# Opening broadcasts placed among squares and projections, weight tiles requested a tile ahead, scan tables two tiles later, in a one-core hybrid block

## The chip, the core and the metric

The kernel runs on one core of a Trainium2 chip. The time is device time in microseconds (us) of one execution. The core has five engines that work through queues of their own, each strictly in order, and wait for each other by semaphores: TensorE (PE in the profile, with its weight loads PEld) for matmuls, VectorE (DVE), ScalarE (ACT), GpSimd (POOL) and SyncE (SP), which here only issues transfers. Matmuls accumulate into PSUM, which has eight banks of 128 x 512 fp32; operands lie in SBUF.

## The reference, cut to what matters

One block over 256 tokens, D = 2048, fp32. The matrices are `w_in` (2048 x 8192), `w_glu`, two output projections, `w_out`, two MLP matrices of 4 x D, and `w_ada`, from which the modulation comes.

```python
mod = silu(c) @ w_ada + b_ada
sh1, sc1, g1, sh2, sc2, g2 = split(mod, 6)
h = rms_norm(x, norm_mix_g) * (1 + sc1) + sh1
u, q, k, v, ga, gb = split(h @ w_in, ...)
y_ssm = s5_branch(u, ...)          # scan, gelu: y; then y * sigmoid(y @ w_glu + b_glu)
y_att = moba_attention(q, k, v, rel_bias)
merged = sigmoid(ga) * (y_ssm @ w_proj_ssm) + sigmoid(gb) * (y_att @ w_proj_attn)
x = x + g1 * (merged @ w_out)
h2 = rms_norm(x, norm_mlp_g) * (1 + sc2) + sh2
x = x + g2 * (square(relu(h2 @ w_ff1)) @ w_ff2)
return rms_norm(x, norm_final_g)
```

## The kernel before

**Products.** Every fp32 product is made of three products in a shorter format: each operand is split into a high part (a cast) and a low part (the difference), and hi x hi, hi x lo and lo x hi are summed. A weight tile is 128 x 1024 fp32, 512 KB. `load` requests it on SP into one of seven buffers (`wraw`, L162 to L167). `split` makes `whi` by a cast on ACT (L172) and `wlo` by a subtraction on DVE (L174); each has four buffers. A tile then feeds either 24 matmuls of 256 columns (`steps_t`, output `pt`, L253 to L255) or 12 of 512 columns (`steps_n`, output `pn`, L309 to L313). `stream` walks over the tiles of a product; where `look` is set, it requests the next tile right after the split of the present one, once.

**Opening.** While x arrives in four pieces, the squares of x are taken on ACT, added up on DVE (`junk`, L520, L521) and summed over the features by matmuls with ones (`ss`, L523), for the norm R. `spread_c(b, gate)` (L1062) writes silu(c), spread over all partitions, into a bank `adab` by four matmuls against the identity; ACT copies it to `cb` (L1070). `cb` is later what DVE multiplies rows of `w_ada` with, to get the modulation as totals (`ada_wide`, L415, 2.3 us each). For the first feature tile the modulation comes from matmuls instead: `ada_first` (`adap`, L343), a copy (`s`, L347) and a transposing product (`adac`, L353). Matmuls that nobody reads (`idle`, L141) stand at the very start and behind `adac`. Then h of the first feature tile is made and the first matmul of the input projection can run.

**Input projection.** `w_in` is worked through by column groups of 1024 and by groups of 1, 3, 4 and 8 feature tiles, as h becomes ready: the list `order` names 15 pieces, and `duo` runs two of them interleaved by a pattern. Partial sums that do not fit into PSUM are copied to SBUF (`qk`, `v`, `uT`, `gp`, all on ACT, L1183) and copied back as seeds (L220: `pn<-v`, `pt<-qk`). The tiles are numbered here from 0 in the order in which they are loaded; tiles 7 to 10 are in the first `duo`, 17 to 27 in the second. h of later feature tiles is made on ACT (`htmp`, L545) and split.

**Attention and scan.** While PE works on the gate columns of `w_in` (four products of 16 tiles), work of the attention heads and then of the state-space scan is put between the tiles by "lanes": lists of jobs that are issued at a given rate per tile. `to_ssm`, called in the second gate product, finishes the heads that are left and puts the list `bgl` of the scan (tables, `ssm_in`, `ssm_scan`, `ssm_ys`, GELU, `hop_out`) in their place. Its end is `yT`, moved between partitions by transfers. `proj_attn(0)` follows (8 tiles of `w_proj_attn`; DVE multiplies the result into `gb`, L1364), then `yT` is split into `yy` (four casts, four subtractions, L172 and L174) and multiplied with `w_glu`.

**What sets the order.** The engines' queues are not written by hand: a scheduler in the framework places every instruction by its own estimate of times, from the order of the program, the priorities (`high_priority`) and the constraints given with `after`. So an edit in one place can move instructions far behind it. Line numbers below are those of the kernel before; in the changed kernel the same operations stand two to eight lines further down or up.

Of the kernel before, what the change touches and what calls it, by code (L numbers as in the profile page):

```python
# [22 lines left out]
KT = D // P  # L23
# [54 lines left out]
class Kern:  # L78
    def __init__(self, ctx, tc, a, out):
        self.tc, self.nc, self.a, self.out = tc, tc.nc, a, out  # L80
        e = ctx.enter_context
        self.cp = e(tc.tile_pool(name="cp", bufs=1))
        self.big = e(tc.tile_pool(name="big", bufs=1))
        self.wp = e(tc.tile_pool(name="wp", bufs=3))
        self.ps = e(tc.tile_pool(name="ps", bufs=1, space=bass.MemoryType.PSUM))
        self.dr = e(tc.tile_pool(name="dr", bufs=1, space=bass.MemoryType.DRAM))
        self.lanes = {}
        self.early = True
        self.last = self.gate = self.hgate = self.agate = None
        self.gates = []  # L90
        self.pend = []
        self.tno = 0
        self.turn = None
        self.done = []
        self.want = lambda kt: None
        self.primed = self.floor = self.force = None
        self.look = self.spare = self.strict = False
        self.cover = True
        self.lead = self.seedgate = None

# [77 lines left out]
    def stream(self, src, kts, c0, homes=()):  # L178
        homes = list(homes)
        kts, nxt = list(kts), None  # L180
        for i, kt in enumerate(kts):
            with self.tc.high_priority(offset=OFF):
                w = nxt if nxt is not None else self.load(src, kt, c0)
                nxt = None
                home = homes.pop(0) if homes else None
                if home:
                    hi, lo = home
                else:
                    hi = self.wp.tile([P, 1024], F32R, name="whi", tag="whi", bufs=4)
                    lo = self.wp.tile([P, 1024], F32R, name="wlo", tag="wlo", bufs=4)  # L190
                self.gate, self.hgate = self.gates.pop(0) if self.gates else (None, None)
                self.tno += 1
                if self.pend and self.pend[0][0] <= self.tno - 2:
                    self.gate = self.pend.pop(0)[1]
                self.split(hi, lo, w)
                self.gate = self.hgate = None
                if self.look:
                    self.look, nxt = False, self.load(src, kts[i + 1], c0)
            if not isinstance(kt, list):
                self.want(kt)  # L200
            yield kt, hi, lo
            self.step()
# [117 lines left out]
    def ada_first(self, j, kt, done, home=None, gate=None):  # L320
        nc = self.nc
        n = 4 * (1 - j) + kt
        st = {}

        def load(i):
            if home is None:
                w = st[i] = self.wp.tile([P, 1024], F32, name="wraw", tag="wraw", bufs=7)
            else:
                w = st[i] = home[i]
            with self.after(self.last):  # L330
                ld = nc.sync.dma_start(w, self.a["wan"][j, kt, i])
            if self.early or home is not None:
                self.last = ld

        def total(i):
            w = st.pop(i).rearrange("p (k n) -> p k n", k=8)
            if i == 0:
                st["p"] = self.aux("adap")
            p = st["p"][:, 0:P]
            with self.after(self.ss_last if self.early else gate):  # L340
                for k in range(8):
                    q = 32 * (k % 4)
                    m = nc.tensor.matmul(p[q:q + 32, :], self.cz[:, 8 * i + k, :], w[:, k, :], start=i == 0 and k < 4,  # L343
                                     stop=i == 1 and k > 3, tile_position=(0, q), skip_group_check=True)
            if i == 1:
                acc = self.s4[:, 512 + P * n:640 + P * n]
                self.acopy = nc.scalar.copy(acc, p)  # L347
                st["acc"], st["last"] = acc, m

        def fold(gate=None):  # L350
            pc = self.tmp("adac")
            with self.after(gate):
                self.adac = nc.tensor.matmul(pc[:, 0:1], st["acc"], self.ones[:, 0:1], start=True, stop=True)  # L353
            done(pc[:, 0:1])
        return ([(lambda i=i: load(i), lambda i=i: total(i)) for i in range(2)], fold, lambda: st["last"])
# [157 lines left out]
    def norm1(self):  # L513
        nc, v = self.nc, self.nc.vector
        x = self.x
        p = self.aux("ss")
        jk = self.slot("S1", [P, 4, 4, S], name="junk")
        for i in range(4):
            with self.after(None if i else self.silu):
                self.squared = nc.scalar.activation(jk[:, i], x[:, 4 * i:4 * i + 4, :], AF.Square)  # L520
            v.tensor_add(jk[:, i, 0:2], jk[:, i, 0:2], jk[:, i, 2:4])  # L521
            for k in range(2):
                m = nc.tensor.matmul(p[:, 0:S], self.ones, jk[:, i, k], start=i + k == 0, stop=i + k == 4)  # L523
            if i in (0, 3):
                self.spread((2, 0, 0, 3)[i], m)
        self.ss_last = m
        s = self.R = self.col("R", S)
        w, u = self.tz0[:, 0:S], self.tz0[:, S:2 * S]
        v.tensor_scalar(w, p[:, 0:S], 1.0 / D, EPS, op0=OP.mult, op1=OP.add)
        self.root = self.nc.scalar.activation(s, w, AF.Abs_reciprocal_sqrt)  # L530
        v.scalar_tensor_tensor(u, s, -0.5, s, op0=OP.mult, op1=OP.mult)
        v.tensor_mul(u, u, w)
        v.scalar_tensor_tensor(s, u, 1.5, s, op0=OP.add, op1=OP.mult)
# [452 lines left out]
    def body(self):  # L986
        nc, a, v = self.nc, self.a, self.nc.vector
        with self.hot():
# [7 lines left out]
            self.eps = self.col("epsc", 1)  # L996
            v.memset(self.eps, EPS)
            self.unread = self.bank("unread")
            self.idle(4)
            self.ident = self.col("ident", P)  # L1000
            make_identity(nc, self.ident)
            nc.scalar.activation(self.col("dum0", 1), self.eps, AF.Silu)
# [41 lines left out]
            return (self.ada_first(1, kt, fin_scale(1, A1, lambda: self.gmix, kt, 1), home and home[0:2], gates[0]),  # L1044
                    self.ada_first(0, kt, fin_shift(0, B1, kt, 1), home and home[2:4], gates[1]))

        def totals(parts):
            for units, fold, last in parts:
                for ld, tot in units:
                    tot()  # L1050
            for units, fold, last in parts:
                fold(parts[1][2]())

        win = a["w_in"][0]
        self.ssm_params()
        with self.tc.high_priority(offset=OF1):
            spread = [self.bank(f"adab{i}") for i in range(4)]

            def spread_c(b, gate):
                for k in range(4 * b, 4 * b + 4):  # L1060
                    with self.after(gate):
                        nc.tensor.matmul(spread[b][:, (k % 4) * P:(k % 4 + 1) * P],  # L1062
                                         rc[:, k:k + 1].to_broadcast([P, P]), self.ident, start=True, stop=True)
            self.spread = spread_c
            for b in range(2):
                spread_c(b, None)
            self.norm1()
            for i in range(4):
                with self.after(self.squared if i < 2 else self.root):
                    nc.scalar.copy(self.cb[:, i * 512:(i + 1) * 512], spread[i])  # L1070
            a2 = self.slot("A2", [P, KT, 2, S], F32R, name="ah")
            self.ah, self.al, self.a2 = a2[:, :, 0], a2[:, :, 1], a2
            parts0 = modn(0)
            for units, fold, last in parts0:
                for ld, tot in units:
                    ld()
            totals(parts0)
            scaled = self.scale1(0, n=1)
            self.idle(6, self.adac)
            h = self.big.tile([P, 2, S], F32, name="htmp", tag="htmp", bufs=1)[:, 0]  # L1080
            v.tensor_scalar(h, x[:, 0], A1[:, 0:1], B1[:, 0:1], op0=OP.mult, op1=OP.add)
            hc = v.tensor_copy(self.ah[:, 0], h)
            h0 = (v.tensor_sub(self.al[:, 0], h, self.ah[:, 0].bitcast(F32)), hc)
            self.done.append(h0)
            self.gates = [(h0[0], self.acopy), h0]
        hv, hq = [self.slot(n, [P, 4, 1024], name="ahm") for n in ("VT", "QT")]
        h4 = [self.slot(n, [P, 2, 1024], name="ahs") for n in ("RT", "S5")]
        regs = [h[:, i, :] for h in (hv, hq) for i in range(4)]
# [158 lines left out]
        def drain(n):  # L1247
            while len(ready) < n:
# [10 lines left out]
        self.lane("ssm", [nop] * SL + self.ssm_builds(), 1.0)  # L1259
        order = [(0, 0, 0), (1, 0, 0), (2, 0, 0), (3, 0, 0), (4, 0, 1), (3, 1, 1), (2, 1, 1), (1, 1, 1), (0, 1, 2),  # L1260
                 (1, 2, 2), (2, 2, 2), (3, 2, 2), (4, 2, 3), (0, 3, 3), (3, 3, 3)]
        def duo(ua, ub, pattern, after, gate=None):
            gens = [(self.steps_n if u[0] in (2, 4) else self.steps_t)(*place(*u), self.ah, self.al,
                                                                     seed=seeds(u[0]) if u[1] else None)
                    for u in (ua, ub)]
            self.strict = True
            banks, todo, ended = [None, None], pattern.count(0), False
            for n, i in enumerate(pattern):
                if i and banks[1] is None:
                    self.spare = True  # L1270
                    self.seedgate = gate and gate()
# [13 lines left out]

        for u, after in zip(order[:3], order[1:4]):
            qkvu(u, after)
        self.look = True
        qkvu(order[3], order[4])
        duo(order[4], order[5], (0, 0, 0, 1, 1, 0, 1), order[6], lambda: h2[0][1])  # L1290
        self.cover = False
        qkvu(order[6], order[7])
        qkvu(order[7], order[8], True)
# [4 lines left out]
        duo(order[12], order[13], (0,) * 8 + (1,) * 4 + (0,) * 4 + (1,) * 4, order[14])  # L1298
        qkvu(order[14])
        self.want = lambda kt: None  # L1300
        self.hop_in()
        qkvu((1, 3, 3), (2, 3, 3))
        self.flush("ssm")
# [34 lines left out]
        for i in range(1, 4):  # L1338
            if i > 1:
                self.lanes["ada"][1] = (RSM, RS2)[i - 2]  # L1340
            dst, c0 = ((ga, 4096), (ga, 5120), (gb, 6144), (gb, 7168))[i]
            banks = self.gemm_n(win, range(KT), c0, self.ah, self.al, mid={8: to_ssm} if i == 1 else {})
            for b in range(4):
                c = (i % 2) * 1024 + (b % 2) * 512
                nc.scalar.copy(dst[:, b // 2, c:c + 512], banks[b])
# [354 lines left out]
```

## Time and profile before

| | |
|---|---|
| median of three runs | 1370.88 us (1370.62 to 1371.35) |
| the profiled execution | 1370.81 us, its span 1369.0 us |
| mean granted clock of TensorE | 0.996 |
| PE busy | 1348.3 us |
| first matmul of the input projection | 18.66 us |
| longest wait of PE after that | 2.8 us, at 57.21 us |
| bytes moved | 356.43 MB, mean 260 GB/s |

A row of the timeline has: start, duration, engine, line, operation, output <- inputs, shape, and how many equal instructions it stands for; in brackets the time that the engine sat idle before it and what ended it. Rows of the table of waits read: who waited <- for whom: total us, times, longest. Rows of the windows have the stretch, then busy time and number of PE, PEld, DVE, ACT and POOL, the granted clock, the DMA share and GB/s.

### The profile page before, as it was taken

Reading aid. Unit: us, or ns where it says so; the run is one execution under the profiler, and the core shown is the slowest. Engines: PE = TensorE matmul, PEld = TensorE weight load, DVE = VectorE, ACT = ScalarE, POOL = GpSimd, SP = SyncE. Lnnn points to the kernel's source line nnn. Section 1 sums busy time; section 2 is a strip of 40 time slices with the busy share of each in tenths; the row PEclk is TensorE's granted clock in tenths of the full one; section 3 lists DMA queues with packets and bytes.
Section 4 is the critical chain, followed back from the end, with each engine's and each line's share of the span. In section 5 each row is a group of like instructions: output and inputs, shape, how many; then the busy total and the mean of one; then the engine's idle time right before and its main releaser. Section 6 shows DMA issues by size and latency. Waiting matters only on the chain.

```text
span 1369.0 us, 21499 instructions
## 1 busy us (share of the span) xinstructions
PE 1348.3 (98%) x8270; PEld 1172.4 (86%) x8270; DVE 1048.8 (77%) x1452; ACT 753.8 (55%) x1048; POOL 40.8 (3%) x91
## 2 busy tenths in 40 slices
PE   9999999999999999999999999999999999999997
PEld 8798899887888888888999888888888888888885
DVE  7788999885997988988887967686766555555676
ACT  7667567567557653455456555454453554535543
POOL 0000004000004000000000000000000000000000
PEclk9999999999999999999999999999999999999998
DMA  9999976895467887988698878888878566566561
GB/s 379 407 409 395 348 226 202 262 331 195 139 211 246 295 306 274 330 335 324 233 344 319 294 229 274 237 254 288 247 246 245 188 188 198 185 187 198 183 199 65
DMA packets 112471, 356.43 MB, mean 260 GB/s; under 512 B 12208, under 2 KB 12352, under 8 KB 111952
## 3 DMA queue, kind: packets, MB, share of 16 engines
q1 hardware_dynamic: 109136, 348.96, 75.1%
q0 software_dynamic: 2800, 5.70, 1.4%
q8 instruction: 65, 1.06, 0.3%
q10 hardware_dynamic: 432, 0.41, 0.1%
q14 instruction: 38, 0.31, 0.1%
HBM read 350.79 MB, written 2.51 MB: 258 GB/s over the span
## 4 chain that ended last, share of the span: by engine, by line
PE 91%; DVE 3%; ACT 3%; DMA 1%; issue 1%; DVEq 0%; ACTq 0%
PE pn L309 17%; PE pn L313 17%; PE pn L311 17%; PE pd L272 13%; PE pd L276 7%; PE pt L255 5%; PE pt L253 5%; PE pt L254 5%; DVE wlo L174 1%; DMA wraw<-in_w_in_dram 1%; ACT whi L172 1%; PE ys L968 1%; PE rk L783 1%; DVE ahm L415 0%; DMA wraw<-in_w_glu_dram 0%
## 5 line engine op out<-in xcount | busy, mean ns | idle before, releaser
L174 DVE TENSOR_TENSOR wlo<-wraw,whi 128x1024 fp32r<-128x1024 f32 x448 | 546.0, 1223 | 246.0 <-ACT whi L172 237.3
L172 ACT CAST whi<-wraw 128x1024 fp32r<-128x1024 f32 x448 | 467.5, 1053 | 469.4 <-PE pn L311 228.7
L272 PE MATMUL pd<-h2h,whi 128*128 128x512 f32 x800 | 209.3, 393 | 0.0
L309 PE MATMUL pn<-whi,ff 128*128 128x512 f32 x496 | 193.0, 389 | 0.0
L311 PE MATMUL pn<-whi,ff 128*128 128x512 f32 x496 | 193.0, 389 | 0.0
L313 PE MATMUL pn<-wlo,ff 128*128 128x512 f32 x496 | 191.6, 389 | 0.0
L272 PEld LDWEIGHTS pd<-h2h,whi 128*128 128x128 f32 x800 | 140.3, 189 | 21.4
L373 DVE SCALAR_TENSOR_TENSOR wraw<-wraw,cb 128x1024 f32<-128x1024 f32 x128 | 156.0, 1219 | 0.0
L309 PE MATMUL pn<-whi,ah 128*128 128x512 f32 x320 | 126.2, 397 | 1.9 <-ACT whi L172 1.0
L276 PEld LDWEIGHTS pd<-h2h,wlo 128*128 128x128 f32 x800 | 116.5, 190 | 12.7
L311 PE MATMUL pn<-whi,ah 128*128 128x512 f32 x320 | 125.5, 392 | 0.0
L276 PE MATMUL pd<-h2h,wlo 128*128 128x256 f32 x800 | 119.8, 281 | 0.0
L313 PE MATMUL pn<-wlo,ah 128*128 128x512 f32 x320 | 113.6, 392 | 0.1
L313 PEld LDWEIGHTS pn<-wlo,ff 128*128 128x128 f32 x496 | 93.1, 188 | 19.4
L309 PEld LDWEIGHTS pn<-whi,ff 128*128 128x128 f32 x496 | 93.1, 188 | 19.2
L311 PEld LDWEIGHTS pn<-whi,ff 128*128 128x128 f32 x496 | 93.1, 188 | 19.0
L253 PE MATMUL pt<-ah,whi 128*128 128x256 f32 x384 | 106.2, 288 | 3.0 <-ACT whi L172 2.8
L254 PE MATMUL pt<-ah,whi 128*128 128x256 f32 x384 | 105.3, 285 | 0.0
L255 PE MATMUL pt<-ah,wlo 128*128 128x256 f32 x384 | 96.0, 287 | 1.0 <-DVE wlo L174 0.8
L253 PEld LDWEIGHTS pt<-ah,whi 128*128 128x128 f32 x384 | 74.0, 194 | 4.6 <-ACT whi L172 3.6
L254 PEld LDWEIGHTS pt<-ah,whi 128*128 128x128 f32 x384 | 74.1, 193 | 0.2
L309 PEld LDWEIGHTS pn<-whi,ah 128*128 128x128 f32 x320 | 60.0, 188 | 15.3 <-ACT whi L172 1.6
(379 smaller groups left out, 2011.6 us busy)
## 6 DMA issues: line engine op xcount, KB each, us to landing
wraw<-in_w_ff_dram SPq DMA_DIRECT2D x256, 512.0 KB, 4.9
wraw<-in_w_in_dram SPq DMA_DIRECT2D x128, 512.0 KB, 5.6
wraw<-in_wat_dram SPq DMA_DIRECT2D x128, 512.0 KB, 5.6
ahm<-in_wat_dram SPq DMA_DIRECT2D x48, 512.0 KB, 8.4
wraw<-in_w_out_dram SPq DMA_DIRECT2D x32, 512.0 KB, 6.2
wraw<-in_w_proj_attn_dram SPq DMA_DIRECT2D x16, 512.0 KB, 5.9
wraw<-in_w_proj_ssm_dram SPq DMA_DIRECT2D x16, 512.0 KB, 6.3
ahm<-in_wan_dram SPq DMA_DIRECT2D x8, 512.0 KB, 10.7
```

Of the source, the lines that this page charges most:

```text
L172: h = self.nc.scalar.copy(hi, src)
L174: s = self.nc.vector.tensor_sub(lo, src, hi.bitcast(F32))
L253: nc.tensor.matmul(o, hi[:, c], xh[:, kx, :], start=st, stop=False, skip_group_check=True)
L254: nc.tensor.matmul(o, hi[:, c], xl[:, kx, :], start=False, stop=False, skip_group_check=True)
L255: self.mm = nc.tensor.matmul(o, lo[:, c], xh[:, kx, :], start=False, stop=sp, skip_group_check=True)
L272: nc.tensor.matmul(banks[blk], hi[:, cut(blk, k)], x2[:, ks[k], :, :], start=i + k == 0, stop=False, skip_group_check=True)
L276: self.mm = nc.tensor.matmul(banks[blk][:, S:2 * S], lo[:, cut(blk, k)], x2[:, ks[k], 0, :], start=False, stop=last and k == 1, skip_group ...
L309: nc.tensor.matmul(o, xh[:, kx, tk], hi[:, c], start=q == 0 and not full, stop=False, skip_group_check=full)
L311: nc.tensor.matmul(o, xl[:, kx, tk], hi[:, c], start=False, stop=False, skip_group_check=full)
L313: self.mm = last = nc.tensor.matmul(o, xh[:, kx, tk], lo[:, c], start=False, stop=q == n - 1, skip_group_check=full)
L373: v.scalar_tensor_tensor(w, w, 1.0, self.cb[:, (i % 2) * 1024:(i % 2 + 1) * 1024], op0=OP.mult, op1=OP.mult, accum_out=pc[:, i:i + 1])
L783: nc.tensor.matmul(p[q, k * 64:(k + 1) * 64], nr[q, i, k].rearrange("p s c -> p (s c)"), self.cc[q, i, 8 * b + k].rearrange("p s c -> p (s ...
```

## The change

It has three parts. In the opening, broadcasts 0 and 1 of silu(c) are issued behind the sums of the first and second square instead of ahead of all of them; broadcast 2 stands between the third and fourth unit of the first `adap` products, and broadcast 3 behind `adac`, in the place of six idle matmuls; nine idle matmuls stand at the start instead of four. The copies of broadcasts 2 and 3 to `cb` are issued after h of the first tile. In the input projection, `look` becomes a number: 1 is the request of one next tile, as before, now also once in the first `duo`; 2 lets every tile from the sixth piece of `order` to the last request its follower ahead. And `to_ssm` is called at tile 10 of the second gate product instead of tile 8.

```diff
-                if self.look:
-                    self.look, nxt = False, self.load(src, kts[i + 1], c0)
+                if self.look and i + 1 < len(kts):
+                    nxt = self.load(src, kts[i + 1], c0)
+                    self.look &= 2
...
-            if i in (0, 3):
-                self.spread((2, 0, 0, 3)[i], m)
+            if i < 2:
+                self.spread(i, m)
...
-            self.idle(4)
+            self.idle(9)
...
+            self.norm1()
+
+            def spread_out(b):
+                with self.after(self.root):
+                    nc.scalar.copy(self.cb[:, b * 512:(b + 1) * 512], spread[b])
             for b in range(2):
-                spread_c(b, None)
-            self.norm1()
-            for i in range(4):
-                with self.after(self.squared if i < 2 else self.root):
-                    nc.scalar.copy(self.cb[:, i * 512:(i + 1) * 512], spread[i])
+                spread_out(b)
...
-            totals(parts0)
+            for n, (ld, tot) in enumerate(parts0[0][0] + parts0[1][0]):
+                tot()
+                if n == 2:
+                    spread_c(2, self.adap_m)
+            for units, fold, last in parts0:
+                fold(parts0[1][2]())
+            spread_c(3, self.adac)
             scaled = self.scale1(0, n=1)
-            self.idle(6, self.adac)
...
+            for b in range(2, 4):
+                spread_out(b)
...
+                if n == early:
+                    self.look = 1
...
-        self.look = True
+        self.look = 1
         qkvu(order[3], order[4])
-        duo(order[4], order[5], (0, 0, 0, 1, 1, 0, 1), order[6], lambda: h2[0][1])
+        duo(order[4], order[5], (0, 0, 0, 1, 1, 0, 1), order[6], lambda: h2[0][1], 4)
+        self.look = 2
...
         self.want = lambda kt: None
+        self.look = 0
...
-            banks = self.gemm_n(win, range(KT), c0, self.ah, self.al, mid={8: to_ssm} if i == 1 else {})
+            banks = self.gemm_n(win, range(KT), c0, self.ah, self.al, mid={10: to_ssm} if i == 1 else {})
```

SP's and POOL's queues hardly change: two loads of the scan's parameters go four transfers later, and one tile of `w_in` goes ahead of one of `w_ada`. The other engines' queues do. On ACT, at the end of the first `duo` (tiles 7 to 12; `gp` is the evacuation of the first gate piece, `pn<-v` and `pt<-qk` are seeds), before:

```order
L172 CAST whi<-wraw 128x1024 x3
L545 ACTIVATE htmp<-xt,B_113,A_112 128x256
L172 CAST ah<-htmp 128x256
L1183 COPY gp<-pn_551 128x512
L1183 COPY gp<-pn_552 128x512
L220 COPY pn_817<-v 128x512
L1183 COPY gp<-pn_553 128x512
L220 COPY pn_818<-v 128x512
L1183 COPY gp<-pn_554 128x512
L172 CAST whi<-wraw 128x1024
L220 COPY pn_819<-v 128x512
L172 CAST whi<-wraw 128x1024
```

and at the same place in the changed kernel:

```order
L173 CAST whi<-wraw 128x1024 x2
L548 ACTIVATE htmp<-xt,B_118,A_117 128x256
L173 CAST ah<-htmp 128x256
L173 CAST whi<-wraw 128x1024 x4
L1187 COPY gp<-pn_550 128x512
L1187 COPY gp<-pn_551 128x512
L222 COPY pn_816<-v 128x512
L1187 COPY gp<-pn_552 128x512
L222 COPY pn_817<-v 128x512
```

The cast of tile 9 moved behind `htmp` and `ah`, those of tiles 10 to 12 moved ahead of all evacuations and seeds. On ACT at the end of the second `duo`, where `pn_1412` and its neighbours are seeds and `qk` evacuations, before:

```order
L172 CAST whi<-wraw 128x1024
L220 COPY pn_1412<-v 128x512
L220 COPY pn_1413<-v 128x512
L1183 COPY qk<-pt_1164 128x512
L172 CAST whi<-wraw 128x1024
L1183 COPY qk<-pt_1165 128x512
L220 COPY pt_1505<-uT 128x4x128
```

and now:

```order
L222 COPY pn_1413<-v 128x512
L222 COPY pn_1414<-v 128x512
L173 CAST whi<-wraw 128x1024
L1187 COPY qk<-pt_1165 128x512
L1187 COPY qk<-pt_1166 128x512
L173 CAST whi<-wraw 128x1024
L222 COPY pt_1506<-uT 128x4x128
```

The cast of tile 27 moved behind two seeds, that of tile 28 behind one more evacuation. On DVE between `proj_attn(0)` and the product with `w_glu`, before:

```order
L373 SCALAR_TENSOR_TENSOR wraw,pc<-wraw,cb 128x1024
L174 TENSOR_TENSOR yy<-yT,yy 128x2x4x64 x3
L1364 TENSOR_TENSOR gb<-gb,pn_4783 128x512
L174 TENSOR_TENSOR yy<-yT,yy 128x2x4x64
L1364 TENSOR_TENSOR gb<-gb,pn_4784 128x512
L1364 TENSOR_TENSOR gb<-gb,pn_4785 128x512
L174 TENSOR_TENSOR wlo<-wraw,whi 128x1024
L373 SCALAR_TENSOR_TENSOR wraw,pc<-wraw,cb 128x1024
```

and now:

```order
L1372 TENSOR_TENSOR gb<-gb,pn_4782 128x512
L175 TENSOR_TENSOR wlo<-wraw,whi 128x1024
L376 SCALAR_TENSOR_TENSOR wraw,pc<-wraw,cb 128x1024
L1372 TENSOR_TENSOR gb<-gb,pn_4783 128x512
L1372 TENSOR_TENSOR gb<-gb,pn_4784 128x512
L1372 TENSOR_TENSOR gb<-gb,pn_4785 128x512
L175 TENSOR_TENSOR wlo<-wraw,whi 128x1024
L175 TENSOR_TENSOR yy<-yT,yy 128x2x4x64 x4
```

The four subtractions of `yy` moved behind all four `gb` products, two `wlo` and one total. On ACT the four casts of `yy` likewise moved behind two more casts of `w_glu` tiles, and on PE the first matmuls of the product became four hi x hi of four banks, followed by one that reads the low part.

More of the change, by code (lines that the diff above doesn't have):

```diff
@@ L96, in __init__ @@
         self.primed = self.floor = self.force = None
-        self.look = self.spare = self.strict = False
+        self.spare = self.strict = False
+        self.look = 0
         self.cover = True
@@ L344, in total @@
                                      stop=i == 1 and k > 3, tile_position=(0, q), skip_group_check=True)
+            self.adap_m = m
             if i == 1:
@@ L1045, in modn @@
                     self.ada_first(0, kt, fin_shift(0, B1, kt, 1), home and home[2:4], gates[1]))
[L1047 to L1052, printed above, removed]
         win = a["w_in"][0]
@@ L1261, in body, with duo @@
                  (1, 2, 2), (2, 2, 2), (3, 2, 2), (4, 2, 3), (0, 3, 3), (3, 3, 3)]
-        def duo(ua, ub, pattern, after, gate=None):
+        def duo(ua, ub, pattern, after, gate=None, early=None):
             gens = [(self.steps_n if u[0] in (2, 4) else self.steps_t)(*place(*u), self.ah, self.al,
@@ L1300, in body @@
         self.want = lambda kt: None
+        self.look = 0
         self.hop_in()
```

## Prediction

> **What bounds the kernel now.** I read the page's busy times and slices first, then its chain, then the table of waits.
>
> ```profile
> PE 1348.3 (98%) x8270; PEld 1172.4 (86%) x8270; DVE 1048.8 (77%) x1452; ACT 753.8 (55%) x1048; POOL 40.8 (3%) x91
> DMA  9999976895467887988698878888878566566561
> PE 91%; DVE 3%; ACT 3%; DMA 1%; issue 1%; DVEq 0%; ACTq 0%
> PE pt L253 <- ACT whi L172: 2.8, 1, 2.8
> PE pn L309 <- ACT whi L172: 1.0, 2, 0.8
> PE pav L863 <- ACT ga L856: 1.7, 1, 1.7
> PE pt L255 <- DVE wlo L174: 0.8, 2, 0.5
> ```
>
> TensorE (PE) works 1348.3 of 1369.0 us and carries 91% of the chain. The number of matmuls hardly changes, so the change can only act on what PE loses between them, some 20 us. The DMA engines are full in the first five slices (9 tenths or more, 170 us), yet no wait of PE in these rows ends on a DMA: each weight tile goes through a cast on ScalarE (ACT, `whi`) and a subtraction on VectorE (DVE, `wlo`), and those are what PE waits for. So I do not ask whether tiles are requested earlier, but where a cast or a subtraction now stands in its in-order queue. Single losses are one of 2.8 us (at 57 us) and many under 1 us. After about 475 us the order of all engines is nearly unchanged and PE does not wait; I cost that stretch at nothing. The same holds for the attention, where I followed the moved rows and found producers ahead of PE, and for the later scan tables: the first groups of the scan stay behind the last head, whose wait (1.7 us, above) stays.
>
> **The opening: -0.6 us.** PE before, and the two additions on DVE that feed the first and the last sum of squares:
>
> ```profile
> 1.06 2.08 PE L141 MATMUL unread<-s 128*128 128x128 f32 x8 [1.06 <-DVE epsc L997]
> 5.19 3.75 PE L1062 MATMUL adab<-ident,tz 128*128 128x128 f32 x16 [2.05 <-ACT tz L1008]
> 8.73 1.50 PE L523 MATMUL ss<-junk,s 128*128 128x256 f32 x4
> 10.07 1.05 PE L1062 MATMUL adab<-ident,tz 128*128 128x128 f32 x8
> 10.96 2.76 PE L523 MATMUL ss<-junk,s 128*128 128x256 f32 x12
> 14.54 1.96 PE L343 MATMUL adap<-wraw,tz 128*32 128x128 f32 x64
> 18.66 0.71 PE L253 MATMUL pt<-ah,whi 128*128 128x256 f32 x4
> 6.02 0.69 DVE L521 TENSOR_TENSOR junk<-junk 128x512 f32<-128x512 f32 x1 [0.76 <-ACT junk L520]
> 10.48 0.68 DVE L521 TENSOR_TENSOR junk<-junk 128x512 f32<-128x512 f32 x1
> ```
>
> The broadcasts at 5.19 run at half rate (16 passes in 3.75 us; later 8 begin 0.89 us ahead of what follows, 0.11 each) and block the first sum, whose data is ready at 6.71. In the new order nine idle matmuls (18 passes of about 0.21 us) fill 1.06 to 4.9, and from 6.71 on sums and two broadcasts alternate. At full rate 16 sum passes (2.76/12 = 0.23) and 16 broadcast passes (0.11) end by 12.1, against 13.5 now: 1.4 us gained. If the rate doubles only near 9.7, where it does now, 3 us at half rate cost 1.5 and nothing is gained; if it again takes 4.4 us of steady work (5.19 to 9.6) counted from 6.71, the sums end near 14.1, a loss of 0.6. One broadcast leaves the stretch ahead of the products and another enters them, about 0.9 us each. The gain lies between -0.6 and +1.4; I take 0.6, halfway from the case of the same moment as now (nearest to these rows) to full rate. The later copies of the third and fourth broadcast (ACT) are hidden behind DMA-fed products.
>
> The Trainium skill, "TensorE: Matmul & The Clock Gate", Part 1, says that the clock starts at half rate and is freed after one busy window of about 3.4 us. The window runs freely. By this rule the nine idle matmuls could free the clock before the first sum, and the 1.4 would be whole; no row of this trace decides it.
>
> **Fourth tile at 29 us: +0.8 us.** ACT's order changes here too: the cast of tile 3 now stands behind the second pair of `v` copies instead of ahead of it, and PE's two `adac` products stand 18 matmuls earlier.
>
> ```profile
> 28.10 1.06 ACT L172 CAST whi<-wraw 128x1024 fp32r<-128x1024 f32 x1
> 29.05 1.09 ACT L1183 COPY v<-pn 128x512 f32<-128x512 f32 x2
> 30.95 0.46 ACT L347 COPY s<-adap 128x128 f32<-128x128 f32 x2
> 29.59 0.39 PE L253 MATMUL pt<-ah,whi 128*128 128x256 f32 x1
> ```
>
> Two copies are 0.95 us at their pace. The cast then ends at 30.1, where PE wants it at 29.59: 0.5 lost. The `adac` products wait for the second `s` copy, now behind the next cast as well (31.5), a further 0.3. Bounds 0.3 and 1.2.
>
> **The stall at 57 us: -2.0 us.** Now four casts (tiles 9 to 12) run right after the modulation of one h tile; before, three of them stood among the evacuations `gp` and the seeds `pn<-v`.
>
> ```profile
> 56.09 1.07 ACT L172 CAST whi<-wraw 128x1024 fp32r<-128x1024 f32 x1
> 64.36 2.96 ACT L172 CAST whi<-wraw 128x1024 fp32r<-128x1024 f32 x3
> 57.19 1.23 DVE L174 TENSOR_TENSOR wlo<-wraw,whi 128x1024 fp32r<-128x1024 f32 x1 [3.85 <-ACT whi L172]
> 68.82 2.35 DVE L174 TENSOR_TENSOR wlo<-wraw,whi 128x1024 fp32r<-128x1024 f32 x2
> 57.21 0.39 PE L253 MATMUL pt<-ah,whi 128*128 128x256 f32 x1 [2.76 <-ACT whi L172]
> 70.83 0.28 PE L255 MATMUL pt<-ah,wlo 128*128 128x256 f32 x1
> 55.00:60.00 5.00, 2.79 (x14) 2.79 (x15) 2.81 (x2) 5.00 (x9) 0.00 (x0) 0.75 1.02 408
> 60.00:65.00 5.00, 5.00 (x27) 4.43 (x27) 5.00 (x5) 4.74 (x10) 0.00 (x0) 0.91 1.03 409
> ```
>
> The stall costs 2.8 us, and the granted clock after it another 5 x 0.25 + 5 x 0.09 = 1.7: 4.5 in all. In the new order the cast of tile 10 ends near 52.6; DVE does tile 9 (to 52.9), a total (2.28, to 55.1) and tile 10 (to 56.3, now 58.4). PE works to 55.3, waits 1 us, and is 3.4 us ahead after tile 10. But it doesn't stay ahead: the cast of tile 13 stands behind some fifteen copies at 0.5 us, ends at 64.3 rather than 65.4, and the subtraction of tile 14 (the first of the pair at 68.82, ends 70.0) comes only 1.1 earlier. PE used it at 70.83, 0.8 later. So 1.1 + 0.8, about 2.0, remains; bounds 1.0 and 4.5.
>
> **At 107 to 128 us: +1.5 us.**
>
> ```profile
> 106.48 1.07 ACT L172 CAST whi<-wraw 128x1024 fp32r<-128x1024 f32 x1
> 107.43 1.13 ACT L220 COPY pn<-v 128x512 f32<-128x512 f32 x2
> 110.12 1.06 ACT L172 CAST whi<-wraw 128x1024 fp32r<-128x1024 f32 x1
> 113.53 1.06 ACT L172 CAST whi<-wraw 128x1024 fp32r<-128x1024 f32 x1
> 114.62 1.23 DVE L174 TENSOR_TENSOR wlo<-wraw,whi 128x1024 fp32r<-128x1024 f32 x1 [2.19 <-ACT whi L172]
> ```
>
> Tile 27's cast moves behind the two seeds (0.95 us later), tile 28's behind one more copy, tile 29's behind one modulation (0.5). PE takes tile 27 as its cast ends, so it loses 1.0. Three bias products, moved ahead of tile 28, fill part of the next wait; tile 29's cast ends near 116.2 (114.6 now) and DVE, which from 114.62 on runs without a pause to 128, is 1.6 late behind it. Bounds 0.4 and 1.7.
>
> **At 464 us: +4.4 us, and +1.7 for the clock.** The move of the scan and the earlier gains reorder the place where the SSM output enters the GLU product (`yy`).
>
> ```profile
> 459.71 3.92 ACT L172 CAST yy<-yT 128x512 fp32r<-128x512 f32 x4
> 462.13 3.14 DVE L174 TENSOR_TENSOR yy<-yT,yy 128x512 fp32r<-128x512 f32 x3
> 466.78 1.27 DVE L1364 TENSOR_TENSOR gb<-gb,pn 128x512 f32<-128x512 f32 x2
> 469.11 1.21 DVE L373 SCALAR_TENSOR_TENSOR wraw<-wraw,cb 128x1024 f32<-128x1024 f32 x1
> 470.86 2.34 DVE L174 TENSOR_TENSOR wlo<-wraw,whi 128x1024 fp32r<-128x1024 f32 x2
> 463.90 0.28 PE L253 MATMUL pt<-yy,whi 128*128 128x256 f32 x1
> ```
>
> Now DVE takes up the `yy` subtractions at 462.13, in time for PE at 463.90. In the new order it first does four `gb` products, two `wlo` and one total: 4 x 0.62 + 2 x 1.17 + 1.15 = 6.0 us from 462.13, when PE's first `pn` bank is done, then the first `yy` (1.05): 469.1. PE's fifth matmul of the product reads it and would be due at 464.4. All rows behind it on PE wait too: 4.7, less the 0.3 that the present order loses here. ACT's two extra casts ahead of `yy` (2 us) end before this. Bounds 3 and 5. Such an idle stretch is longer than the one at 57, so I add the 1.7 of clock found there; bounds 0 and 3. The same page and part say that an idle window of about 3.4 us throttles again; the rows at 55 and 60 agree, and the sum is the same.
>
> **Sum.** -0.6 + 0.8 - 2.0 + 1.5 + 4.4 + 1.7 = +5.8 us on the profiled run's 1370.81 (its span 1369.0 and 1.8 around it; the median of three is 1370.88): **1376.6**.
>
> **Rivals.**
> (A) The clock holds at 464, as it does through the 1.7 us wait of `pav`: 1374.9. Against it: that wait is a third as long.
> (B) On the other side: PE finds `yy` ready at 464. One place, price 6.1: 1370.5, not slower. It decides itself by DVE's queue: if the first `yy` subtraction starts before about 463.3 in the present times. For it: DVE has idle time elsewhere and the other tiles' work may run before the `gb` products can. Against it: the queue is in order, and the `gb` product at its head needs PE's last tile but a few matmuls.
> (C) The stall at 57 goes whole and stays gone (4.5 instead of 2.0), with the opening's whole 1.4: 1376.6 - 2.5 - 0.8 = 1373.3. For it: DVE's idle 3.85 goes with it. Against it: tile 13's cast.
> (D) B and C together: 1367.2.
> (E) The clock rule alone frees the opening early: 1375.8.
>
> **How the numbers follow.** Forecast 0.46, A 0.15, B 0.16, C 0.10, D 0.08, E 0.05. About 0.2% (2.7 us) is what a measurement of this kernel can tell from no change. D and a little of B's spread lie below 1368.1: faster 0.10. The rest of B and nearly all of C lie within: 0.23. What is left, 0.67, is slower. The range 1369.0 to 1380.0 takes in B, and above the forecast the bounds of the clock and the opening (+3.4 together); it leaves out D and a tail above.
>
> **What would show it.** Right: PE idle 4 to 5 us at the first `pt<-yy`, ended by DVE `yy`, with a PEclk below 1 behind it; the stall at 57 down to 1 us with full clock; a wait of 1 us for `whi` near 107; the first `pt` at about 18.0. Wrong: no such wait at 464, then B; a first `pt` at 17.2, then the clock was free early; PE more than 3 us ahead at 71 us, then C.

## The result, and the profile after

The changed kernel takes 1382.97 us (median of 4 runs, 1380.76 to 1384.34) against 1370.75 us before on the same chip (1370.46 to 1371.35): a ratio of 1.0087, 95% interval 1.0070 to 1.0105. It is slower, by about 12 us, twice what was forecast. Its profiled execution took 1384.34 us with a span of 1382.5, 13.5 us longer than that of before.

That execution is the slowest of the four. From the page of the changed kernel: busy times, the granted clock in 40 slices, and the chain of work that ended last.

```profile
PE 1354.3 (98%) x8268; PEld 1175.9 (85%) x8268; DVE 1048.4 (76%) x1452; ACT 755.2 (55%) x1048; POOL 40.8 (3%) x91
PEclk9999999999999899999999999999999999999999
PE 86%; DVE 5%; ACT 5%; DMA 3%; issue 1%; SPq 0%; DVEq 0%; ACTq 0%
```

TensorE's share of the chain falls from 91 to 86%; DVE and ACT have 5% each instead of 3. Its busy time is 6.0 us longer with one idle matmul (two passes) fewer: a part of the matmuls ran at half rate, and one slice (the 14th, 449 to 484 us) has a clock under 9 tenths. The table of PE's waits in the changed kernel (us in total, times, longest) names the places:

```profile
PE pt L255 <- ACT yy L173: 3.4, 1, 3.4
...
PE pt L256 <- DVE yy L175: 1.9, 1, 1.9
PE pav L866 <- ACT ga L859: 1.7, 1, 1.7
PE rk L786 <- issue: 1.6, 1, 1.6
...
PE pt L255 <- ACT whi L173: 1.4, 2, 0.8
...
PE pn L311 <- ACT ah L173: 0.8, 1, 0.8
```

The wait of 2.8 us for `whi` is gone. New are `yy` (3.4 and 1.9), `rk` and `ah`. To see what each is worth I compare when the same `pt` and `pn` products start in two traces (median over those that start in the 4 us from the time given, in us of before; + is later):

| at (us of before) | after | opening alone (1) | `early` alone (2) | `look = 2` alone (3) | tables alone (4) |
|---|---|---|---|---|---|
| 18.6 | +0.85 | -0.81 | -0.44 | +0.55 | +0.62 |
| 32 | +1.81 | +0.18 | -0.44 | +0.54 | +0.62 |
| 54 | -0.98 | +0.19 | -3.22 | +0.55 | +0.62 |
| 100 | -1.00 | -0.65 | -3.25 | +0.73 | +0.86 |
| 120 | +0.14 | -0.67 | -3.25 | +1.88 | +0.86 |
| 178 | +1.66 | -0.67 | -3.27 | +3.40 | +0.85 |
| 325 | +3.51 | -0.66 | -3.25 | +4.84 | +0.87 |
| 446 | +4.93 | -0.65 | -3.23 | +4.83 | +2.31 |
| 510 | +13.49 | -0.05 | -3.53 | +4.61 | +8.97 |
| 1200 | +13.46 | -0.05 | -3.53 | +4.57 | +8.99 |

The column "after" is the result place by place: +0.85 in the opening, +0.96 by the fourth tile, -2.8 at 57 us, +1.1 at 107, **+1.5 at 177**, **+1.9 at 247**, **+1.4 at 341**, +8.5 at `yy`, and nothing behind. The last four columns are the experiments below; each column is one traced execution.

**The place of `yy`.** PE, ACT and DVE of the changed kernel in order of time (start, duration, instruction, idle before and what ended it):

```profile
472.40 1.22 PE L255 MATMUL pt<-yy,whi 128*128 128x256 f32 x4 [3.41 <-ACT yy L173]
475.54 0.58 PE L256 MATMUL pt<-yy,whi 128*128 128x256 f32 x1 [1.91 <-DVE yy L175]
464.09 2.13 ACT L173 CAST whi<-wraw 128x1024 fp32r<-128x1024 f32 x2 [2.17 <-DMA wraw<-in_w_glu_dram]
467.73 1.05 ACT L173 CAST whi<-wraw 128x1024 fp32r<-128x1024 f32 x1 [1.51 <-PE pn L315]
470.29 1.04 ACT L173 CAST whi<-wraw 128x1024 fp32r<-128x1024 f32 x1 [1.50 <-DMA wraw<-in_w_glu_dram]
471.24 3.91 ACT L173 CAST yy<-yT 128x512 fp32r<-128x512 f32 x4
467.45 1.22 DVE L376 SCALAR_TENSOR_TENSOR wraw<-wraw,cb 128x1024 f32<-128x1024 f32 x1
468.59 0.68 DVE L1372 TENSOR_TENSOR gb<-gb,pn 128x512 f32<-128x512 f32 x1
469.19 1.22 DVE L175 TENSOR_TENSOR wlo<-wraw,whi 128x1024 fp32r<-128x1024 f32 x1
470.33 1.22 DVE L376 SCALAR_TENSOR_TENSOR wraw<-wraw,cb 128x1024 f32<-128x1024 f32 x1
471.47 1.88 DVE L1372 TENSOR_TENSOR gb<-gb,pn 128x512 f32<-128x512 f32 x3
473.27 1.22 DVE L175 TENSOR_TENSOR wlo<-wraw,whi 128x1024 fp32r<-128x1024 f32 x1
474.40 4.12 DVE L175 TENSOR_TENSOR yy<-yT,yy 128x512 fp32r<-128x512 f32 x4
```

Both queues are as the order showed them, but ACT is late too. Its two casts of `w_glu` tiles ahead of `yy` were priced at 2 us of work; they also wait, 1.51 us for PE to free a `whi` buffer and 1.50 us for the second one's tile to land. So PE waits first for ACT's cast (3.41), works four products, and waits for DVE's subtraction (1.91). It is DVE that sets when PE gets past this place: from 467.45 on it has no gap, its first `yy` subtraction ends at 475.5 (the first of the four in the last row), and the product that reads it starts at 475.54. An earlier ACT cast would let PE do the four products earlier and wait longer for DVE.

**At 177 us** the modulation of the last features stands behind casts. ACT and PE in the changed kernel, then ACT before:

```profile
172.76 1.06 ACT L173 CAST whi<-wraw 128x1024 fp32r<-128x1024 f32 x1 [0.91 <-PE pn L313]
173.72 1.09 ACT L548 ACTIVATE htmp<-xt,B,A 128x256 f32<-128x256 f32 x2
175.53 1.05 ACT L173 CAST whi<-wraw 128x1024 fp32r<-128x1024 f32 x1 [0.72 <-ACT htmp L548]
176.48 0.61 ACT L173 CAST ah<-htmp 128x512 fp32r<-128x512 f32 x1
177.15 1.19 PE L311 MATMUL pn<-whi,ah 128*128 128x512 f32 x4 [0.80 <-ACT ah L173]
```

```profile
169.39 1.10 ACT L545 ACTIVATE htmp<-xt,B,A 128x256 f32<-128x256 f32 x2 [6.31 <-DVE B L1028]
171.33 0.61 ACT L172 CAST ah<-htmp 128x512 fp32r<-128x512 f32 x1
```

The cast of `ah` comes 5.2 us later, and `ah` had been ready only some 4 us ahead of its use.

**At 247 us** (`rk`, the products behind the scan's tables), PE and DVE of the changed kernel, then PE before:

```profile
240.83 4.93 PE L786 MATMUL rk<-cc,tt 64*64 64x64 f32 x161
247.34 2.89 PE L786 MATMUL rk<-cc,tt 64*64 64x64 f32 x91 [1.58 <-issue]
242.84 4.53 DVE L792 SCALAR_TENSOR_TENSOR rt<-rk,rmask,rt 128x512 f32<-128x512 f32 x8 [1.45 <-PE rk L786]
```

```profile
244.94 7.89 PE L783 MATMUL rk<-cc,tt 64*64 64x64 f32 x256
```

Before, all 256 `rk` products run in one piece without a pause; now they start 4.8 us earlier and PE pauses 1.58 us among them. The profile names no releaser, and DVE, which empties their banks, is not it by the times: PE goes on as DVE ends its eight operations here (247.37), but 0.5 us ahead of that end in run 3 and 0.7 us behind it in run 11. What fits is the transfer of instructions (queue q8, "instruction" on the page of the profile: 65 transfers of 16 KB, about one for every 127 of PE's matmuls). In the five profiles with this pause (1.2 to 2.3 us) the first such transfer among the `rk` products lands 1.3 to 1.6 us before PE goes on; in the eight without it, it lands 0.5 to 2.8 us before the first `rk` product. So PE probably waits for its own instructions, because the short `rk` products (7.89/256 = 0.03 us each) now come ahead of that transfer; no run here tests this.

### The profile page after: what moved, and what is told of

It reads as the page before. It is cut to its first block, busy times and chain, and to the rows that moved or that the text cites. A ratio compares the mean times of both kernels' runs of the same rounds, so it can differ in the third digit from the quotient of the medians.

```text
span 1382.5 us, 21498 instructions
## 1 busy us (share of the span) xinstructions
PE 1354.3 (98%) x8268; PEld 1175.9 (85%) x8268; DVE 1048.4 (76%) x1452; ACT 755.2 (55%) x1048; POOL 40.8 (3%) x91
## 4 chain that ended last, share of the span: by engine, by line
PE 86%; DVE 5%; ACT 5%; DMA 3%; issue 1%; SPq 0%; DVEq 0%; ACTq 0%
PE pn L311 16%; PE pn L313 16%; PE pn L315 16%; PE pd L274 13%; PE pd L278 7%; PE pt L257 5%; PE pt L255 5%; PE pt L256 5%; DMA ahm<-in_wat_dram 1%; ACT whi L173 1%; DVE wlo L175 1%; DVE ahm L418 1%; DMA wraw<-in_w_in_dram 1%; PE rk L786 1%; DMA wraw<-in_w_glu_dram 1%
```

## The experiments

Each kernel was timed beside the kernel before; its difference is given to the median of before on the same occasion (1370.91 us for 1 to 4, 1370.33 for 5 to 8, 1370.54 for 9 to 11), and its ratio with the 95% interval. The change falls into four parts that can be had alone: the opening, `early`, `look = 2` and the tables (`mid`). Theory S is what the table above suggests: each part has its own places and prices, and they add up.

**1. The opening alone.** Before, with all of the change's edits to the opening, of which the core is

```diff
-            if i in (0, 3):
-                self.spread((2, 0, 0, 3)[i], m)
+            if i < 2:
+                self.spread(i, m)
...
-            self.idle(4)
+            self.idle(9)
```

> Only the new order of the opening, everything else as before. Theory S (each part costs what its own rows show, and the parts add up): the first pt product starts 0.8 us later (19.4 instead of 18.7), the second tile another 0.3 and the fourth tile 0.7 more, so +1.8 us at 35 us into the span and, if the stall at 57 us absorbs none of it, 1372.5. Theory I (the loss of 12 us is an interaction, no part costs much alone): within 0.5 us of 1370.8. The opening step of the prediction: -0.6 in the opening and +0.8 at the fourth tile, 1371.0.

1371.2 us, +0.3 (ratio 1.0003, 0.9993 to 1.0012): the prediction's two steps together, less than theory S. The trace shows the first `pt` product 0.8 us *earlier* than before, where the changed kernel with the same opening has it 0.85 later. PE's first rows in this run, then in the changed kernel:

```profile
1.06 4.10 PE L142 MATMUL unread<-s 128*128 128x128 f32 x18 [1.06 <-DVE epsc L1000]
6.49 1.13 PE L526 MATMUL ss<-junk,s 128*128 128x256 f32 x4 [1.34 <-DVE junk L524]
```

```profile
1.05 4.21 PE L142 MATMUL unread<-s 128*128 128x128 f32 x18 [1.05 <-DVE epsc L1000]
6.84 2.08 PE L526 MATMUL ss<-junk,s 128*128 128x256 f32 x4 [1.57 <-DVE junk L524]
```

The same four products take 1.13 us here and 2.08 there: by the trace's record of the clock, the rate doubles at 4.9 us in this execution and at 10.6 in the other. So one profile cannot price the opening. The +1.0 between 18.6 and 32 us in the table is there in both; it gives back what the earlier clock wins.

**2. `early` alone.**

```diff
-        duo(order[4], order[5], (0, 0, 0, 1, 1, 0, 1), order[6], lambda: h2[0][1])
+        duo(order[4], order[5], (0, 0, 0, 1, 1, 0, 1), order[6], lambda: h2[0][1], 4)
```

> Only the one early request inside the first interleaved pair of units (look = 1 from its fifth step). Theory S: the wait of 2.8 us for whi at 57 us shrinks to about 1 us, the half clock behind it goes, 3.4 us are won there and about 2.7 kept: 1368.1. The prediction's step kept 2.0: 1368.8. Theory I: no gain alone, 1370.8, since the subtraction of the later tiles is late either way.

1368.24 us, -2.7 (0.9977, 0.9968 to 0.9987): the part that gains, and faster than both kernels. In its trace PE waits 0.65 us at 55.9 and 0.49 us at 67.7 us, both for `wlo`, with full clock. Of the 2.8 us won there nothing is lost again up to the end.

**3. `look = 2` alone.**

```diff
+        self.look = 2
         self.cover = False
         qkvu(order[6], order[7])
...
         self.want = lambda kt: None
+        self.look = 0
```

> Only the lasting early request (look = 2 from the seventh unit to the fifteenth). Theory S: 1.2 us lost at 107 us, 1.5 at 177 us (PE waits for the last features of ah, whose modulation stands behind five more casts on ACT), 1.9 at the rk products near 247 us: +4.6 without a change of the clock at the wait of pav near 341 us, +6.0 with it; 1375.4 or 1376.8. No wait at the first yy product. The prediction's step: +1.5, 1372.4. Theory I: within 1 us of 1370.8.

1375.67 us, +4.8 (1.0038, 1.0023 to 1.0053), as theory S has it without a lost clock at 341. Its waits hold the two that the prediction did not have:

```profile
PE rk L785 <- issue: 1.2, 1, 1.2
...
PE pn L311 <- ACT ah L173: 0.8, 1, 0.8
```

**4. The tables alone.**

```diff
-            banks = self.gemm_n(win, range(KT), c0, self.ah, self.al, mid={8: to_ssm} if i == 1 else {})
+            banks = self.gemm_n(win, range(KT), c0, self.ah, self.al, mid={10: to_ssm} if i == 1 else {})
```

> Only the scan's tables two tiles later. Theory S: the whole order at the yy product comes from here: waits of 3.4 and 1.9 us ended by ACT yy and DVE yy, half clock behind them, +8.5 us: 1379.3 (7 to 9 us). The prediction took the order from this move and the earlier gains together, 4.4 + 1.7: 1376.9. Theory L (the wait came from the later weight tile's landing, because the earlier requests had filled the DMA queues): alone it costs under 3 us.

1378.76 us, +7.9 (1.0048, 1.0032 to 1.0065). Both waits are there, without any early request:

```profile
PE pt L255 <- ACT yy L173: 3.0, 1, 3.0
...
PE pt L256 <- DVE yy L175: 1.9, 1, 1.9
```

Theory L falls. The four parts alone add up to +0.3 - 2.7 + 4.8 + 7.9 = +10.3 us, against +12.2 for all; the intervals of the parts are wide enough for the rest. In the traces the clock has a hand in it: at `yy` 8.5 us are lost with three windows of 3.41 us at half rate in the changed kernel, and 6.7 us with two in run 4.

**5. `yy` ahead in both queues.** The changed kernel; the third cast of a `w_glu` tile waits for the last `yy` split, and the `gb` products (taken out of `proj_attn` into `attn_mul`) for its subtraction.

```diff
+        self.gates = [(None, None)] * 2 + [self.done[-1]]
+        attn_mul(0, pa, self.done[-1][0])
         banks = self.gemm_t(a["w_glu"][0], range(8), 0, yy[:, 0], yy[:, 1])
```

> The changed kernel, with the four yy casts ahead of the third w_glu cast on ACT and the four yy subtractions ahead of the gb products on DVE (by an order constraint; same instructions). Theory S (the loss at the first yy product is made by the order of these two queues, and the lateness of yT itself, which lands by 464.1 us, costs little): no wait over 1 us and no half clock there, 7 to 8.5 us won: 1374 to 1376. Theory T (yT's own landing, 10 us later than before, is what ends the wait): the casts start at most 1 us earlier and under 3 us are won, 1380 or more.

1377.64 us, +7.3 (1.0044, 1.0029 to 1.0059): about 5 us of the changed kernel's 12 gone, less than theory S said, more than theory T allows. In its trace (1374.5 us, the fastest of four) the waits for `yy` and the half clock are gone; the loss at this place is 2.0 us (8.5 in the changed kernel). In their stead stands

```profile
PE pt L255 <- DVE gb L1375: 1.8, 1, 1.8
```

which is a wait that my own order made: the products of `yy` need a PSUM bank that a `gb` product empties, and all four now stood behind the subtractions.

**6. Work during the wait.** The tables alone (4), and

```diff
+        for _ in range(24):
+            with self.after(mm):
+                nc.tensor.matmul(warm[:, 0:S], yh[:, 0, 0:P], yl[:, 1, :], start=True, stop=True)
         banks = self.gemm_t(a["w_glu"][0], range(8), 0, yy[:, 0], yy[:, 1])
```

> Scan tables two tiles later, nothing else, plus 24 products of 0.12 us into an unused bank between the last proj_attn product and the first yy product, so that TensorE works through most of its wait of 3.0 us (2.9 us of extra work). If half clock after the wait is a price of its own (theory S: two windows of 3.4 us at half rate in the run with the later tables, about 2 to 2.5 us beyond the waits), it goes or shrinks to one window and the time falls to 1376 to 1377 although nothing else is faster. If the wait alone is the price, the time stays at 1378.8 or rises by what the extra products overrun.

1378.05 us, +7.7 (1.0050, 1.0035 to 1.0065): no gain over run 4, not the 1376 to 1377 that was expected. The trace says why:

```profile
464.25 3.03 PE L1383 MATMUL warm<-yl,yh 128*128 128x256 f32 x24
470.27 0.38 PE L256 MATMUL pt<-yy,whi 128*128 128x256 f32 x1 [2.31 <-DVE yy L175]
```

The first wait is filled, but the second one, for DVE's subtraction, is 2.31 us instead of 1.9 and takes the clock by itself, for one window of 3.41 us. About 6.7 us are lost here, as in run 4. DVE is the bound of this place; what PE did until then was worth nothing.

**7 and 8. Longer work at the start.** Run 2 with more idle products, and run 1 with more:

```diff
-            self.idle(4)
+            self.idle(10)
```

```diff
-            self.idle(9)
+            self.idle(14)
```

> Before, with the one early request alone, and ten idle products instead of four at the start, so that TensorE works without a gap from 1.05 us to the first broadcasts at 5.1. If the clock is freed at the end of the first full window of about 3.4 us of work on a grid that runs freely (the profiles so far freed it at 6.8 to 11.1 us, and three changes of clock in the changed kernel's trace lie on one grid of 3.41 us), it is freed between 4.5 and 7.9 us, always before the first sum of squares ends: first pt at 17.7 to 18.2 (18.2 to 19.3 in the four profiles with four idle products), 0.5 to 1 us won: 1367.4. If it is freed at a fixed moment near 9.7 us, or idle products do not count, nothing is won: 1368.2.

> Only the new order of the opening, with 14 idle products instead of 9 (work without a gap from 1.05 us until the first sum of squares, near 6.8). Grid theory: nine idle products cover 4.0 us, so a whole window falls into them only in some executions (the two profiles so far freed the clock at 10.4 and at 6.8 or earlier); 14 always cover one, so the clock is free by 7.9 us in every execution, first pt at 17.8, and the spread of the times shrinks: 1370.6 with a range under 2.5 us. Fixed-moment theory: as with nine, 1371.2.

Both did what they were to do to the clock, which is free at 4.35 and 4.57 us (8.9 in run 2); PE's first sums in run 7, and its wait at the fourth tile:

```profile
6.74 1.03 PE L525 MATMUL ss<-junk,s 128*128 128x256 f32 x4
...
28.93 0.39 PE L255 MATMUL pt<-ah,whi 128*128 128x256 f32 x1 [0.52 <-ACT whi L173]
```

The first `pt` product is 1.27 and 0.79 us earlier than in before. Yet the times are 1367.72 (-2.6; 0.9981, 0.9971 to 0.9991) and 1371.32 (+1.0; 1.0004, 0.9994 to 1.0013): neither can be told from the run with fewer idle products, and run 8's times spread over 3.2 us, not under 2.5. The traces show why: the lead does not last to 32 us. There run 7 is 0.57 us early and run 2 0.44, since in run 7, too, the fourth tile's cast stands behind the second pair of `v` copies; run 8 is 0.18 us late, as run 1 is.

**9. All but the tables.** The changed kernel with run 4's edit taken back.

```diff
-            banks = self.gemm_n(win, range(KT), c0, self.ah, self.al, mid={10: to_ssm} if i == 1 else {})
+            banks = self.gemm_n(win, range(KT), c0, self.ah, self.al, mid={8: to_ssm} if i == 1 else {})
```

> The changed kernel with the scan's tables started at the earlier tile again (opening and both early requests kept). If the parts add up (theory S), the loss at the first yy product goes whole: the three remaining parts alone gave +0.3, -2.7 and +4.8, which is 1373.1 on 1370.7. If the earlier requests were a cause of the wait too (theory L), some of it stays: over 1377.

1373.61 us, +3.1 (1.0027, 1.0017 to 1.0038), as the sum of the parts said; no wait for `yy`.

**10. `look = 2` for one pair only.** Run 3, with

```diff
         duo(order[8], order[9], (0,) * 5 + (1,) * 2 + (0,) * 2 + (1,) * 2, order[10])
         self.lanes["ssm"][1] = SR1
+        self.look = 0
```

> The lasting early request ended after the second interleaved pair of units, nothing else changed. It tells which pair costs what: theory S says that this pair costs the wait near 107 us alone (+1.2 us, of the prediction's +1.5), and that the losses at 177 and 247 us (1.5 and 1.9 us), which the prediction cost at nothing, come from the third pair: 1371.6. If the losses at 177 and 247 us come from the weights' ring being ahead since 107 us, they stay: 1375.2.

1372.06 us, +1.5 (1.0013, 1.0003 to 1.0023). In its trace the products go from 0.28 us early at 100 us to 0.85 late at 120, as in run 3, and stay there to 458; the waits for `ah` and `rk` are gone. The losses at 177 and 247 us come from the third pair.

**11. `yy` ahead, `gb` between.** Run 5, with one `gb` product behind the second, third and fourth subtraction each, and the last behind all.

```diff
             self.split(sc4(yy[:, 0, 2 * k:2 * k + 2]), sc4(yy[:, 1, 2 * k:2 * k + 2]), yT[:, 2 * k:2 * k + 2])
+            if k:
+                attn_mul(0, pa, k - 1, self.done[-1][0])
```

> The changed kernel with the yy casts ahead of the third w_glu cast, as in the run before with that order, but with the gb products between the yy subtractions (two yy, gb, yy, gb, yy, gb, gb) instead of behind them. In that run a new wait of 1.8 us had come in: TensorE's yy products wait for a bank that the gb product behind the subtractions frees. If that is all that was left, it goes: no wait over 1 us at the first yy product, loss there under 0.7 us (8.5 in the changed kernel, 2.0 in that run), 1375.5. If yT's lateness still binds, a wait for ACT yy or DVE yy of over 1 us shows there.

1375.24 us, +4.7 (1.0028, 1.0017 to 1.0040); its trace also has the longest pause among the `rk` products, 2.3 us, with a window at half rate behind it. At the `yy` products 0.6 us are lost, and the wait for the bank has become

```profile
PE pt L255 <- DVE gb L1374: 0.2, 1, 0.2
```

So nearly 8 of the 8.5 us were the order of two queues. Which of the two is not separated by runs 5 and 11, which change both; that it is DVE's rests on the rows above and on run 6. That `yT` comes some 10 us later with the later tables costs under 1 us here by itself (0.6 us lost, where run 9, with the earlier tables, gains 0.3).

## Why the prediction was right in sign and wrong in size

It had the bound right (PE, through the place of casts and subtractions in two in-order queues), the sign, and the largest term's place and mechanism. The forecast of +5.8 became +12.2, above its range. Of the 7.7 us between +5.8 and the profiled execution's +13.5, 3.4 lie in a stretch that was costed at nothing, 2.5 at `yy` (most of it the clock), 1.4 in a loss of the clock at 341 us and 1.5 in the opening; the other steps come out 1.0 better than forecast together. (The +3.4 above the forecast that the range ascribes to the clock and the opening is 2.5 by these steps' own bounds, 1.3 and 1.2.) Step by step:

- **The opening: forecast -0.6, +0.85 in this profile.** The step took the moment at which the rate doubles ("near 9.7, where it does now") for a property of the kernel. It changes with the execution: 8.9 to 11.1 us in the six profiles with the old opening, and with the new one 4.1 to 5.9 us in four (first `pt` 0.8 to 1.15 us earlier than in before's profile) and 10.6 in the fifth, that of the changed kernel. So the nine idle products do free the clock mostly, as rival E had it, and this profile fell on the other side by luck.
- **Fourth tile: +0.8, measured +1.0** (+0.7 there, the rest a cast behind a copy to `cb` in the second tile, which had been called hidden). With the usual opening the two terms cancel, as run 1 shows.
- **The stall at 57 us: -2.0, measured -2.8**, and run 2 shows it alone. The mechanism was right, the size cautious: of the 3.4 us of lead 0.6 was given back at tiles 13 and 14, not the 1.4 reckoned. The slices of the changed kernel, with full clock:

```profile
55.00:60.00 5.00, 4.36 (x31) 3.92 (x30) 5.00 (x4) 5.00 (x10) 0.00 (x0) 1.00 1.03 411
60.00:65.00 5.00, 5.00 (x25) 4.16 (x24) 4.97 (x8) 5.00 (x10) 0.00 (x0) 1.00 1.02 406
```

- **At 107 us: +1.5, measured +1.1** (run 10 the same, run 3 1.15). Right.
- **"The same holds for the attention, where I followed the moved rows and found producers ahead of PE"** and the cost of nothing for the rest between 128 and 464 us: wrong by 3.4 us (1.5 at 177 us, 1.9 at 247; in run 3 3.0, in run 10 nothing). The third pair was read for its weights, which do come earlier; what else moves with them, the modulation of `ah` behind the earlier casts and the `rk` products on PE, was not costed. For `ah` this was the same reasoning that the prediction used at 107 us, left out one pair later.
- **`yy`: +4.4 and +1.7, measured 5.0 (3.41 + 1.91 less the 0.34 lost here before) and 3.6.** The mechanism was right: from its first `gb` product to the end of its first `yy` subtraction DVE takes 6.9 us without a gap, against 7.0 reckoned. Two terms were mis-sized. The first is the clock, for which the price of the stall at 57 us, one window at half rate, was carried over: this wait reaches into three windows, and 7.29 us of work in them at half rate (row below) is 3.6 us. The second is DVE's start, taken to stay at 462.13: it is 468.59, which is 463.7 in times of before (PE is 4.9 us late there), since two `wlo` and a total ahead of it wait for casts of `w_glu` tiles, the first of which waits 2.17 us for its tile to land. "ACT's two extra casts ahead of `yy` (2 us) end before this" left out their waits for a buffer and a landing, 3.0 us; PE's first wait comes of that, but DVE's ends later and covers it. The prediction also laid the reordering on "the move of the scan and the earlier gains" together; run 4 shows the move alone, and run 11 the cure. Its reading that the rows at 55 and 60 us agree with what it cites there from the Trainium skill holds only loosely: the wait in them was 2.76 us (see the last paragraph).
- **The clock at 341 us: not foreseen, +1.4.** Rival A leant on the wait of `pav`, through which the clock had held, and the prediction let that wait "stay" at no cost. It holds there by chance: in three of the thirteen profiles it does not (next section but one).

## What to carry to other kernels

When a request or a cast is put earlier in an in-order queue, price what now stands behind it, at every place where the rule applies, as carefully as what it serves: here one early request gained 2.7 us, and the same request made a habit lost 4.8. A cast that is put ahead must be priced with its waits (buffer and landing), not with its duration; but what a place costs is set by the queue that ends last, here DVE's, not by the one that is waited for first. Keep the single request, and try a queue's order at the consumer (run 11) before blaming the lateness of the data.

## What the runs showed of the hardware

In all thirteen traces the granted clock changes only on a grid of 3.41 us, whose phase differs from execution to execution. In windows cut along that grid (PE busy time is the second number, PEclk the third from the end), first the changed kernel at 341 and at 468 us, then before at 337 us, then run 1 at the stall of 57 us:

```profile
341.66:345.07 3.41, 1.73 (x19) 1.27 (x18) 0.00 (x0) 3.41 (x8) 0.11 (x1) 1.00 0.00 0
345.07:348.48 3.41, 3.41 (x61) 3.29 (x58) 1.57 (x3) 1.73 (x4) 0.00 (x0) 0.50 0.00 0
467.95:471.36 3.41, 1.04 (x5) 0.54 (x3) 3.41 (x5) 1.91 (x3) 0.00 (x0) 1.00 1.02 399
471.36:481.60 10.24, 7.29 (x32) 6.99 (x33) 7.69 (x11) 4.84 (x5) 0.00 (x0) 0.50 0.57 211
481.60:485.01 3.41, 3.41 (x31) 3.41 (x29) 2.12 (x4) 1.05 (x1) 0.00 (x0) 1.00 0.42 137
```

```profile
337.32:340.74 3.42, 1.72 (x10) 1.25 (x9) 0.00 (x0) 3.41 (x7) 0.00 (x0) 1.00 0.00 0
340.74:344.15 3.41, 3.41 (x73) 2.79 (x71) 1.66 (x3) 2.71 (x7) 0.11 (x1) 1.00 0.00 0
```

```profile
52.70:56.11 3.41, 1.94 (x9) 1.28 (x7) 0.83 (x2) 2.79 (x6) 0.00 (x0) 1.00 1.04 414
56.11:59.53 3.42, 2.09 (x15) 1.89 (x16) 2.15 (x2) 3.42 (x6) 0.00 (x0) 1.00 1.02 407
59.53:62.94 3.41, 3.41 (x21) 3.03 (x21) 3.41 (x4) 3.41 (x7) 0.00 (x0) 1.00 1.03 407
```

A window at full clock in which PE works little is followed by one at half rate. In the thirteen traces this happened after every one with 1.32 us of work or less out of 3.41, and after none with 1.82 or more; of nine with 1.66 to 1.76 us, four lost the clock and five kept it. So the limit lies near half, and the record of PE's work does not place it closer: the same 1.7 us wait of `pav`, with 1.72 us of work in its window, kept the clock in before and lost it, with 1.73, in the changed kernel. At half rate, the opening included, windows with 2.82 us of work or more ended it and windows with 2.70 or less did not, so a wait that reaches into the next window holds the clock down for longer. The stall of 2.76 us at 57 us lost the clock in before; in run 1 it fell across a boundary, left 1.94 and 2.09 us of work on its two sides, and cost no clock. So a wait under 3.4 us has two prices, its length and, by the phase, up to 1.7 us more for each window at half rate. That this is also what spreads the times of one kernel was not shown: one execution of each was traced.

The Trainium skill, "TensorE: Matmul & The Clock Gate", Part 1, has this window of 3413 ns and says that it runs freely and that the clock is freed after a busy one; these traces agree, to the window's length. It puts the return to half rate at an idle window of about 3.4 us; here 1.68 us of idle time in one window was enough.
